# A two-layer window and differential attention encoder: first-layer input chunks 1 to 3 read in rows and turned on TensorE, and a planned wait of the mask step narrowed

## The chip, the core and the metric

The kernel runs on one core of a Trainium2 chip. The metric is the device time of one execution in microseconds; the time before is the median of 3 runs. The engines are TensorE (PE: matmuls and transposes; its weight loads are PEld), VectorE (DVE), ScalarE (ACT), GpSimd (POOL) and the queue of SyncE (SP), from which every DMA is issued in order.

## What is computed

Two sequences (1024 and 512 tokens, each with 16 meta tokens ahead, 1568 rows of 1024 together) pass through two layers. Cut to what matters:

```python
def layer(x, ...):
    h = rmsnorm(x, pre_g)                       # over the 1024 columns
    proj = h @ w_in                             # 3328 columns
    aq, ak, av, ag, bq, bk, bv, bg = split(proj)
    # A: 8 heads of 64, 2 key heads, window of +-128 tokens, meta keys, a sink
    oa = window_gqa_attention(rope(aq), rope(ak), av, sink) * silu(ag)
    # B: 4 heads, two softmaxes over all keys, p0 - lam * p1, then a norm
    ob = diff_attention(rope(bq), rope(bk), bv, lam, ...) * silu(bg)
    return x + rmsnorm(concat(oa, ob) @ w_out, post_g)
```

In the window attention the scores outside the window are masked with -1e30 ahead of the softmax.

## The kernel before

**Chunks and products.** The 1568 rows are cut into four chunks of up to 392 tokens (`ICH`; the copy of the 16 meta rows is left out). A product in full precision is three passes: each operand is split into a rounded part `hi` and a rest `lo`, and `hi*hi`, `lo*hi`, `hi*lo` are summed in one PSUM tile. `dense` makes one block of 128 output columns for one chunk: 8 slices of the contraction by 3 passes, 24 matmuls of up to 392 columns into `ps_d` (or `ps_o` where that is free). A head's input projection is four such blocks (`whl`, `whl`, `kk` and `vv` hold the first head's four weight blocks; the third is its values, the fourth its gate). `project` evicts each block with rope, split and DMA stores: `BS` (queries and keys), `BV` and `AV` (values in token rows, a quarter of a chunk on each partition range), `GT` (gates).

**Chunks of the first layer.** `load_x` reads every chunk from the transposed input `xT`, model dimension on the partitions. `start_stats` calls `prestats` for it: squares (ACT or POOL), sums on DVE, four PE transposes, a DVE reduction, two small POOL steps for the power -0.5, four more PE transposes (`rstd_bc`) and a copy to `rb`. `prenorm` then multiplies each of the eight slices by the gain and by `rb` on DVE (into `at`), and splits it: `hi` by a copy on ACT or DVE, `lo` by a subtraction on DVE. Chunk 0 goes another way: it is split without its norm, and `rb` is multiplied in at the eviction.

**Second layer.** `pre` works on token rows: `stat` sums squares on ACT, the rows are scaled, then groups of four PE transposes turn them into `ps_t`, and `hi` and `lo` come straight from that PSUM tile with the gain.

**Attention.** `attn_b` (B heads, four units) fills `ps_s` with scores, takes minima, exponentials and sums, transposes the probabilities (`pp` to `ps_t` to `at`) and multiplies by the values (`vv`). `attn_a` (two units) takes the heads in batches of three that share one `ps_s` tile of three banks; each head is two matmuls, then a DVE mask step (`tensor_tensor_reduce`: adds the mask and takes the minimum), an exponential and, per query block, `attn_a_tail`. Its result goes out as `MX`. `outproj` runs in steps (`OUT_ORDER`): `b` is the half of the products that needs only B heads, `s` and `S` the half that needs A heads, `p` the residual, `n` is `pre`.

**What sets the order.** Nothing is issued as written. `Recorder` notes every operation with what it reads and writes, and `schedule` is a list scheduler over the five engines with a priced duration for each operation: among the ready ones the smallest priority number goes first (`seq` less `boost` and `base`). An operation with two forms (`any`, `any_copy`) goes to the engine that is free. The engines then run these fixed orders, and the semaphores come from the data. `nc.extra` adds dependencies that only this planning sees. All instructions carry the helper's line (451 before, 448 after), so rows are told apart by their tiles.

Of the kernel before, what the change touches and what calls it, by code (L numbers as in the profile page):

```python
# [16 lines left out]
ALU = mybir.AluOpType  # L17
# [16 lines left out]
    [[(0, 392)], [(392, 392)], [(784, 256), (1056, 120)], [(1176, 392)]],  # L34
# [18 lines left out]
QUICK = 1  # L53
# [5 lines left out]
PRE_ACT = (0, 0, 0, 0, 0, 0, 0, 0)  # L59
# [4 lines left out]
ONLY = 4  # L64
# [478 lines left out]
def hymba_kernel(ctx, tc, xT, xr, w_in, w_out, rope, masks, pre_g, post_g, sub_g, sink_b, sink_m, lam_in, yo):  # L543
# [64 lines left out]
    def load_x(ci):  # L608
        xin[ci] = pair()
        nc.boost = START[f"x{ci}"] * 100000  # L610
        w = 2 if ci == 0 else 4
        for k in range(0, 8, w):
            o = 0
            for t0, m in ICH[0][ci]:
                dma(xin[ci][k // 4][:, k % 4:k % 4 + w, o:o + m],
                    xT.rearrange("(a p) t -> p a t", p=128)[:, k:k + w, t0:t0 + m])
                o += m
        nc.boost = 0
# [104 lines left out]
    def prestats(xs, tmp, n, only=False):  # L723
        if only:
            for i in range(4):
                r = slice(2 * (i % 2), 2 * (i % 2) + 2)
                x, y = xs[i // 2][:, r, 0:n], tmp[i // 2][:, r, 0:n]
                nc.any((nc.scalar, "activation", (y, x, AF.Square), {}),
                       (nc.gpsimd, "tensor_tensor", (y, x, x), dict(op=ALU.mult)))
                if i:  # L730
                    nc.vector.tensor_tensor(
                        tmp[0][:, 0:2, 0:n], tmp[0][:, 0:2, 0:n], tmp[i // 2][:, r, 0:n], op=ALU.add)
            nc.vector.tensor_tensor(tmp[0][:, 0, 0:n], tmp[0][:, 0, 0:n], tmp[0][:, 1, 0:n], op=ALU.add)
        else:
            for i in range(2):
                nc.scalar.activation(tmp[i][:, :, 0:n], xs[i][:, :, 0:n], AF.Square)
            nc.any_tt(tmp[0][:, :, 0:n], tmp[0][:, :, 0:n], tmp[1][:, :, 0:n], ALU.add)
            for k in (2, 1):
                nc.any_tt(tmp[0][:, 0:k, 0:n], tmp[0][:, 0:k, 0:n], tmp[0][:, k:2 * k, 0:n], ALU.add)
        return rstd_bc(tmp[0][:, 0, 0:n], n, 1.0 / D)  # L740

    def scaled(out, x, g, rb, n, act):
        for j in range(x.shape[1]):
            if act:
                nc.scalar.activation(out[:, j, 0:n], x[:, j, 0:n], AF.Copy, scale=g[:, j:j + 1])
                nc.any_tt(out[:, j, 0:n], out[:, j, 0:n], rb[:, 0:n], ALU.mult)
            else:
                nc.vector.scalar_tensor_tensor(
                    out[:, j, 0:n], x[:, j, 0:n], g[:, j:j + 1], rb[:, 0:n], op0=ALU.mult, op1=ALU.mult)

    def prenorm(l, ci, xs, rb, n):
        his, los = [], []
        for i in range(2):
            hi, lo = pair(F32R)
            for j in range(4):
                r = slice(j, j + 1)
                h = at_p([128, 1, CN])
                scaled(h, xs[i][:, r], preg[:, l, 4 * i + j:4 * i + j + 1], rb, n, PRE_ACT[2 * ci + i])
                h = h[:, :, 0:n]
                nc.any_copy(hi[:, r, 0:n], h)  # L760
                if l == 0 and ci < QUICK:
                    nc.vector.tensor_tensor(lo[:, r, 0:n], h, f32(hi[:, r, 0:n]), op=ALU.subtract)
                else:
# [834 lines left out]
```

## Time and profile before

| what | value |
|---|---|
| time, median of 3 runs (range) | 1935.77 us (1933.12 to 1939.91) |
| the profiled execution's own time | 1938.61 us |
| its span | 1936.8 us |
| PE busy | 1843.4 us, 95% of the span |
| DVE, ACT, POOL busy | 1515.2, 1008.1, 279.3 us |
| mean granted TensorE clock | 0.985 |

The profiled execution has its own time: 1.8 us of it lie outside the span. A sum made from the trace is a change against 1938.61, and is then taken from the median. A busy PE need not be PE at its peak, so durations of matmuls are read here from one start to the next. "Idle before" in a timeline is the wait just ahead of the row, with what ended it.

### The profile page before, as it was taken

The page shows a single profiled execution, that of the slowest core. Times are in us where ns is not written, and L with a number is a line of the kernel's source. Part 1 is how long each engine was busy: PE and PEld are TensorE (multiplying, and loading weights), DVE is VectorE, ACT ScalarE, POOL GpSimd, SP SyncE. Part 2 cuts the span into 40 slices and gives each one's busy share as a digit, 9 for nine tenths or more (in the row PEclk, how much of TensorE's full clock was granted, in tenths as well). Part 3 has the DMA queues.
Part 4 walks back from the last instruction along what each step waited for, and adds up shares of the span by engine and source line. Part 5 has one row for each costly group of instructions (what it writes and reads, how often), then busy time and mean ns, then how long its engine had stood idle before and what let it go on. Part 6 is the DMA issues. An engine that isn't in the chain of part 4 may idle for free.

```text
span 1936.8 us, 35552 instructions
## 1 busy us (share of the span) xinstructions
PE 1843.4 (95%) x12328; PEld 1771.3 (91%) x12328; DVE 1515.2 (78%) x3363; ACT 1008.1 (52%) x2417; POOL 279.3 (14%) x516
## 2 busy tenths in 40 slices
PE   6999999999999989999789999999999999999998
PEld 5989989999989889999789999999999999889998
DVE  8858788888787787587988397787967859869767
ACT  4335445454444475575765254454545438648632
POOL 3001111211121210000221021121111101101001
PEclk8999999999999999999989999999999999999999
DMA  7253363544543657556354535445353475684464
GB/s 252 56 161 105 110 170 102 148 119 109 153 117 108 154 144 198 118 133 178 120 196 116 152 100 160 120 118 161 98 167 114 124 180 125 159 229 99 109 205 150
DMA packets 299147, 273.02 MB, mean 141 GB/s; under 512 B 101560, under 2 KB 263480, under 8 KB 298840
## 3 DMA queue, kind: packets, MB, share of 16 engines
q1 hardware_dynamic: 298968, 270.75, 50.5%
q8 instruction: 98, 1.61, 0.4%
q14 instruction: 81, 0.66, 0.1%
HBM read 149.19 MB, written 96.01 MB: 127 GB/s over the span
## 4 chain that ended last, share of the span: by engine, by line
PE 70%; DVE 11%; DMA 8%; ACT 4%; issue 4%; SPq 2%; POOL 1%; DVEq 0%; POOLq 0%; ACTq 0%
PE ps_d L451 43%; PE ps_s L451 10%; PE ps_o L451 9%; PE ps_t L451 8%; DVE at L451 2%; DVE pp L451 2%; DVE slot L451 2%; ACT pp L451 2%; SPq L451 2%; DVE sm L451 1%; DMA vv<-BV 1%; DVE og L451 1%; DMA kk<-AK 1%; DVE ru L451 1%; POOL sm L451 1%
## 5 line engine op out<-in xcount | busy, mean ns | idle before, releaser
L451 PE MATMUL ps_d<-slot,whl 128*128 128x392 f32 (+2 forms) x4560 | 938.2, 347 | 15.0 <-ACT slot L451 6.7
L451 PEld LDWEIGHTS ps_d<-slot,whl 128*128 128x128 f32 x4560 | 785.7, 190 | 22.2 <-ACT slot L451 6.7
L451 PE MATMUL ps_s<-kk,qq 128*128 128x264 f32 (+9 forms) x1496 | 284.4, 319 | 21.7 <-ACT pp L451 5.7
L451 PE MATMUL ps_o<-at,vv 128*128 128x256 f32 (+6 forms) x1368 | 285.9, 307 | 8.4 <-DVE og L451 5.5
L451 ACT ACTIVATE at<-ps_t 128x256 fp32r<-128x256 f32 (+9 forms) x434 | 187.7, 439 | 202.7 <-PE ps_t L451 177.4
L451 ACT ACTIVATE pp<-ps_s,sm 116x1040 f32<-116x1040 f32 (+4 forms) x208 | 203.9, 980 | 169.9 <-DVE sm L451 161.5
L451 DVE TENSOR_TENSOR at<-ps_t,at 128x256 fp32r<-128x256 f32 (+6 forms) x472 | 224.5, 480 | 68.0 <-ACT at L451 53.5
L451 PEld LDWEIGHTS ps_s<-kk,qq 128*128 128x128 f32 (+4 forms) x1496 | 227.2, 185 | 46.9 <-ACT pp L451 9.0
L451 PE MATMUL ps_d<-whl,slot 128*128 128x256 f32 x1800 | 259.0, 288 | 8.6 <-DVE slot L451 6.0
L451 PEld LDWEIGHTS ps_d<-whl,slot 128*128 128x128 f32 x1800 | 235.1, 192 | 14.3 <-DVE slot L451 7.2
L451 DVE TENSOR_REDUCE sm<-ps_s 116x1 f32<-116x1040 f32 (+4 forms) x208 | 218.3, 1050 | 34.3 <-PE ps_s L451 33.3
L451 ACT ACTIVATE pp<-pp,sm 128x336 f32<-128x336 f32 (+6 forms) x347 | 206.6, 607 | 61.0 <-DVE sm L451 57.6
L451 PEld LDWEIGHTS ps_o<-at,vv 128*128 128x128 f32 (+1 forms) x1368 | 214.0, 190 | 16.8 <-ACT pp L451 5.4
L451 PE MATMUL ps_t<-ident,pp 128*128 128x128 f32 (+6 forms) x1248 | 203.5, 269 | 3.1 <-DVE at L451 1.6
L451 POOL TENSOR_TENSOR pad<-pp,pad 128x64 fp32r<-128x64 f32 (+3 forms) x145 | 53.2, 370 | 819.0 <-ACT pad L451 528.1
L451 PEld LDWEIGHTS ps_t<-ident,pp 128*128 128x128 f32 (+6 forms) x1248 | 147.8, 137 | 14.7 <-ACT pp L451 2.8
L451 DVE CUSTOM_DVE_ANT_0 pp<-ps_s,mk,nsinks 128x336 f32<-128x336 f32 (+2 forms) x192 | 97.1, 528 | 22.1 <-PE ps_s L451 20.3
L451 POOL TENSOR_TENSOR sm<-sm 128x2 f32<-128x2 f32 (+3 forms) x112 | 48.7, 437 | 408.2 <-DVE sm L451 404.6
L451 POOL TENSOR_TENSOR sm<-sm,mhalf 128x1 f32<-128x1 f32 (+7 forms) x98 | 80.8, 830 | 132.9 <-DVE sm L451 129.6
L451 ACT ACTIVATE og<-ps_o 64x128 f32<-64x128 f32 (+4 forms) x248 | 66.1, 287 | 44.8 <-PE ps_o L451 27.3
L451 ACT ACTIVATE ru<-ps_d 128x392 f32<-128x392 f32 (+5 forms) x100 | 48.7, 487 | 73.9 <-PE ps_d L451 64.2
L451 DVE TENSOR_TENSOR slot<-slot 128x512 f32<-128x512 f32 (+3 forms) x79 | 73.9, 945 | 8.4 <-ACT slot L451 8.0
(158 smaller groups left out, 2130.3 us busy)
## 6 DMA issues: line engine op xcount, KB each, us to landing
wraw<-in_w_in_dram SPq DMA_DIRECT2D x46, 512.0 KB
qq<-qq SPq DMA_DIRECT2D x144, 128.0 KB
BS<-st SPq DMA_DIRECT2D x80, 196.0 KB
qq<-AQ SPq DMA_DIRECT2D x96, 128.0 KB
gl<-GT SPq DMA_DIRECT2D x72, 128.0 KB
MX<-og SPq DMA_DIRECT2D x72, 128.0 KB
slot<-MX SPq DMA_DIRECT2D x11, 768.0 KB
kk<-BS SPq DMA_DIRECT2D x8, 1040.0 KB
```

Source lines behind the costliest of these rows:

```text
L451: fn(*[_real(a) for a in args], **{k: _real(a) for k, a in kw.items()})
```

## The change

Chunk 0 is loaded as before. Chunks 1 to 3 are read from `xr`, the input in token rows, as four tiles each of 96 or 98 rows by 1024 columns (chunk 3 into `pp` tiles, the others into `slot` tiles). Their norm is now `stat`, moved out of `outproj`: two ACT squares with a running sum per tile, one small DVE step and one POOL power; the rows are scaled in place (ACT or DVE). `turned`, which `pre` of the second layer now calls too, makes the transposes, `hi` and `lo`. Chunk 1 ends at 776 in place of 784, so that chunks 1 and 2 have 384 tokens (four times 96). In `attn_a` the line that made the planner hold the three mask steps of a batch until the batch's last matmul is gone. The planner's price of a DMA now follows the number of rows.

```diff
-    [[(0, 392)], [(392, 392)], [(784, 256), (1056, 120)], [(1176, 392)]],
+    [[(0, 392)], [(392, 384)], [(776, 264), (1056, 120)], [(1176, 392)]],
...
+        for v in (out, in_):
+            rows = [x for x in v.shape if x > 1] or [1]
+            nc.weight = max(nc.weight, cost * 16 // max(k for k in range(1, 17) if rows[0] % k == 0))
...
+            for j in range(4):
+                nc.stream = "x" if ci == 3 else "dense"
+                x = (p_p if ci == 3 else slot)([128, 2, 512])
...
+                    dma(x[a:b].rearrange("p u d -> p (u d)"), xr[t0:t0 + b - a])
...
+    def stat(parts, M):
+        r = sm_p([128, 4])
+        for u, p in enumerate(parts):
+            sq = ru_p([128, 512])
+            nc.scalar.activation(sq[0:M], p, AF.Square, scale=1.0 / 32, accum_out=r[0:M, u:u + 1])
+        nc.vector.scalar_tensor_tensor(
+            r[0:M, 2:3], r[0:M, 0:1], EPS, r[0:M, 1:2], op0=ALU.add, op1=ALU.add)
+        nc.gpsimd.tensor_tensor(r[0:M, 3:4], r[0:M, 2:3], mhalf[0:M, 0:1], op=ALU.pow)
+        return r[0:M, 3:4]
+
+    def turned(l, tiles, off, n):
+        his, los = [], []
+        for u in range(2):
+            hi, lo = pair(F32R)
+            for k in range(4):
+                pt = ps_t([128, 512])
+                o = 0
+                with nc.macro():
+                    for get, M in tiles:
+                        nc.tensor.transpose(
+                            pt[:, o:o + M], get(u)[:, 128 * k:128 * k + 128], ident[0:M, 0:M])
+                        o += M
+                g = preg[:, l, 4 * u + k:4 * u + k + 1]
+                p = pt[:, off:off + n]
+                nc.any_copy(hi[:, k, 0:n], p, g)
                 nc.vector.scalar_tensor_tensor(
...
+                    lo[:, k, 0:n], p, g, f32(hi[:, k, 0:n]), op0=ALU.mult, op1=ALU.subtract)
...
-                nc.extra = [nc.last]
                 for bi, (u, i) in enumerate(batch):
...
+            for x in xin[ci]:
+                r = stat([x[0:n // 4, u] for u in range(2)], n // 4)
+                for u in range(2):
+                    nc.any_copy(x[0:n // 4, u], x[0:n // 4, u], r)
```

PE in the first projection, before, after the matmuls of chunk 0 for all four blocks; `ps_t<-ident,slot` and `ps_t<-ident,sm` are the two groups of `rstd_bc`:

```order
L451 MATMUL ps_d<-slot,vv 128x392 x18
L451 MATMUL ps_t<-ident,ru 98x128 x4
L451 MATMUL ps_t<-ident,slot 98x128 x4
L451 MATMUL ps_t<-ident,sm 128x98 x4
L451 MATMUL ps_t<-ident,slot 94x128 x4
L451 MATMUL ps_o<-slot,whl 128x392 x3
```

The same place in the changed kernel; the groups of four or eight with `128x96` are the new transposes of chunk 1:

```order
L448 MATMUL ps_d<-slot,whl 128x392 x15
L448 MATMUL ps_t<-ident,sm 128x98 x4
L448 MATMUL ps_d<-slot,whl 128x392 x9
L448 MATMUL ps_o<-slot,kk 128x392 x12
L448 MATMUL ps_t<-ident,slot 128x96 x8
L448 MATMUL ps_o<-slot,kk 128x392 x12
L448 MATMUL ps_d<-slot,whl 128x384 x3
```

Chunk 1 now follows three blocks of chunk 0; the fourth block (`vv`) comes for all chunks behind chunk 3.

ACT at the start, before; `whl`, `kk`, `vv` from `pp` are the `hi` parts of the weights, `slot<-slot` the squares of chunks 0 and 1:

```order
L451 ACTIVATE slot<-slot 128x784 x3
L451 ACTIVATE slot<-slot,preg 128x392 x2
L451 ACTIVATE slot<-slot 128x784 x2
L451 ACTIVATE whl<-pp 128x1024
L451 ACTIVATE kk<-pp 128x1024
L451 ACTIVATE vv<-pp 128x1024
```

The same place on ACT in the changed kernel; `ru,sm<-slot` are the squares with their sums, `slot<-slot,sm` the scaling of rows:

```order
L448 ACTIVATE slot<-slot,preg 128x392 x2
L448 ACTIVATE ru,sm<-slot 96x512 x8
L448 ACTIVATE slot<-slot,sm 96x512
L448 ACTIVATE kk<-pp 128x1024
L448 ACTIVATE rb<-ps_t 128x392
L448 ACTIVATE slot<-slot,sm 96x512 x6
L448 ACTIVATE ru,sm<-slot 96x512
L448 ACTIVATE slot<-ps_t,preg 128x384 x2
```

Eight squares of chunk 1 stand ahead of the third weight block and of `rb`.

PE at the end of the first layer's attention, before; `ps_o<-at,vv` is the last product of the window attention, `ps_t<-ident,slot` are the transposes of `pre` for the second layer:

```order
L451 MATMUL ps_o<-at,kk 128x256
L451 MATMUL ps_d<-whl,slot 128x256 x3
L451 MATMUL ps_o<-at,vv 128x512
L451 MATMUL ps_d<-whl,slot 128x256 x12
L451 MATMUL ps_t<-ident,slot 128x128 x12
L451 MATMUL ps_d<-whl,slot 128x256 x30
```

The same place in the changed kernel:

```order
L448 MATMUL ps_o<-at,kk 128x256
L448 MATMUL ps_d<-whl,slot 128x256 x6
L448 MATMUL ps_o<-at,vv 128x512
L448 MATMUL ps_d<-whl,slot 128x256 x6
L448 MATMUL ps_d<-whl,at 80x256 x12
L448 MATMUL ps_d<-whl,slot 128x256 x12
```

150 output matmuls (eight short rows of three and one of 99 follow those shown) stand between the last product and the first transpose, where 12 stood; the transposes come behind them.

## Rows read from the trace of the kernel before

**Rows 1.** The page: engines over the span, last chain by engine, one group (busy, mean ns).
```profile
PE 1843.4 (95%) x12328; PEld 1771.3 (91%) x12328; DVE 1515.2 (78%) x3363; ACT 1008.1 (52%) x2417; POOL 279.3 (14%) x516
...
PE 70%; DVE 11%; DMA 8%; ACT 4%; issue 4%; SPq 2%; POOL 1%; DVEq 0%; POOLq 0%; ACTq 0%
...
L451 PE MATMUL ps_t<-ident,pp 128*128 128x128 f32 (+6 forms) x1248 | 203.5, 269 | 3.1 <-DVE at L451 1.6
```

**Rows 2.** Windows by stage: length, busy of each engine, granted clock, DMA.
```profile
0.00:119.00 119.00, 97.76 (x517) 92.70 (x517) 88.95 (x161) 43.52 (x72) 22.62 (x22) 0.94 0.54 170
...
650.00:962.00 312.00, 291.87 (x2119) 276.90 (x2119) 249.53 (x736) 203.68 (x584) 33.48 (x64) 0.98 0.58 148
962.00:1097.00 135.00, 120.38 (x788) 117.41 (x787) 94.26 (x176) 65.01 (x133) 21.43 (x29) 0.94 0.53 162
...
1850.00:1937.00 87.00, 74.57 (x599) 72.75 (x597) 60.84 (x97) 24.70 (x59) 10.84 (x12) 0.96 0.49 168
```

**Rows 3.** Timeline of PE, first stage: start, length, instructions, idle before.
```profile
9.05 7.27 PE L451 MATMUL ps_d<-slot,whl 128*128 128x392 f32 x22 [1.66 <-DVE slot L451]
...
40.28 0.91 PE L451 MATMUL ps_t<-ident,sm 98*128 98x98 f32 x4 [5.76 <-POOL sm L451]
...
44.81 1.18 PE L451 MATMUL ps_d<-slot,whl 128*128 128x392 f32 x3
45.79 1.18 PE L451 MATMUL ps_d<-slot,kk 128*128 128x392 f32 x3
...
60.70 4.53 PE L451 MATMUL ps_d<-slot,vv 128*128 128x392 f32 x24
65.06 0.68 PE L451 MATMUL ps_d<-slot,whl 128*128 128x376 f32 x3
...
73.29 0.60 PE L451 MATMUL ps_t<-ident,slot 128*98 128x128 f32 x4
73.64 0.76 PE L451 MATMUL ps_d<-slot,whl 128*128 128x376 f32 x3
...
118.69 0.28 PE L451 MATMUL ps_s<-kk,qq 128*116 128x264 f32 x1
```

**Rows 4.** Groups by form, 0 to 160 us: DVE steps of `prenorm` (busy, mean ns).
```profile
L451 DVE SCALAR_TENSOR_TENSOR at<-slot,preg,rb 128x392 f32<-128x392 f32 x16 | 9.2, 618 | 2.4 <-ACT rb L451 2.4
...
L451 DVE TENSOR_TENSOR slot<-at,slot 128x392 fp32r<-128x392 f32 x16 | 8.4, 557 | 0.3 <-ACT slot L451 0.2
```

**Rows 5.** Timeline of ACT near 945 us: one square with its sum, from `stat`.
```profile
944.98 0.62 ACT L451 ACTIVATE ru<-slot 128x512 f32<-128x512 f32 x1
945.50 0.18 ACT L451 ACTIVATION_READ_ACCUMULATOR ru<-slot 128x1 f32 x1
```

**Rows 6.** Windows of 1 us: a 98-row store of `BV`, then the 94-row stores.
```profile
47.00:48.00 1.00, 1.00 (x4) 1.00 (x4) 1.00 (x3) 0.91 (x3) 0.00 (x0) 0.50 0.87 256
96.00:97.00 1.00, 1.00 (x7) 1.00 (x7) 1.00 (x2) 0.00 (x0) 0.00 (x0) 1.00 0.14 48
```

**Rows 7.** Timeline of PE between the layers.
```profile
961.05 1.59 PE L451 MATMUL ps_d<-whl,slot 128*128 128x256 f32 x12
...
970.42 1.59 PE L451 MATMUL ps_t<-ident,slot 128*128 128x128 f32 x6 [7.57 <-ACT slot L451]
975.50 1.09 PE L451 MATMUL ps_t<-ident,slot 128*128 128x128 f32 x4 [3.49 <-DVE slot L451]
...
979.55 5.82 PE L451 MATMUL ps_d<-whl,slot 128*128 128x256 f32 x28 [1.16 <-DVE slot L451]
```

**Rows 8.** Timeline of SP: the store of the window attention's last result.
```profile
968.73 0.37 SPq L451 DMA_DIRECT2D MX<-og  x1
```

**Rows 9.** Timeline of PE, second layer's end.
```profile
1847.51 13.97 PE L451 MATMUL ps_d<-whl,slot 128*128 128x256 f32 x114
1863.14 0.38 PE L451 MATMUL ps_d<-kk,slot 128*128 128x256 f32 x1 [1.66 <-ACT kk L451]
```

**Rows 10.** Waits of DVE over the span: us, times, longest.
```profile
DVE pp L451 <- PE ps_s L451: 30.8, 19, 8.1
```

More of the change, by code (lines that the diff above doesn't have):

```diff
@@ L608, in load_x @@
     def load_x(ci):
-        xin[ci] = pair()
+        n = sum(m for _, m in ICH[0][ci])
         nc.boost = START[f"x{ci}"] * 100000
[L611 to L617, printed above, removed]
+        if ci == 0:
+            xin[0] = pair()
+            for k in range(0, 8, 2):
+                dma(xin[0][k // 4][:, k % 4:k % 4 + 2, 0:n],
+                    xT.rearrange("(a p) t -> p a t", p=128)[:, k:k + 2, 0:n])
+        else:
+            m = n // 4
+            cols = [t0 + i for t0, k in ICH[0][ci] for i in range(k)]
+            xin[ci] = []
+            for j in range(4):
+                nc.stream = "x" if ci == 3 else "dense"
+                x = (p_p if ci == 3 else slot)([128, 2, 512])
+                a = 0
+                while a < m:
+                    t0, b = cols[m * j + a], a
+                    while b < m and cols[m * j + b] == t0 + b - a:
+                        b += 1
+                    dma(x[a:b].rearrange("p u d -> p (u d)"), xr[t0:t0 + b - a])
+                    a = b
+                nc.stream = "dense"
+                xin[ci].append(x)
         nc.boost = 0
@@ L721, in rows @@
         return [t[:, j] for t in tiles for j in range(k)]
[L723 to L739, printed above, removed]
-        return rstd_bc(tmp[0][:, 0, 0:n], n, 1.0 / D)
@@ L742, in scaled, with prestats @@
[L742 to L747, printed above, removed]
-                nc.vector.scalar_tensor_tensor(
[L749 to L763, printed above, removed]
-                    nc.any_tt(lo[:, r, 0:n], h, f32(hi[:, r, 0:n]), ALU.subtract)
+    def prestats(xs, tmp, n):
+        for i in range(4):
+            r = slice(2 * (i % 2), 2 * (i % 2) + 2)
+            x, y = xs[i // 2][:, r, 0:n], tmp[i // 2][:, r, 0:n]
+            nc.any((nc.scalar, "activation", (y, x, AF.Square), {}),
+                   (nc.gpsimd, "tensor_tensor", (y, x, x), dict(op=ALU.mult)))
+            if i:
+                nc.vector.tensor_tensor(
+                    tmp[0][:, 0:2, 0:n], tmp[0][:, 0:2, 0:n], tmp[i // 2][:, r, 0:n], op=ALU.add)
+        nc.vector.tensor_tensor(tmp[0][:, 0, 0:n], tmp[0][:, 0, 0:n], tmp[0][:, 1, 0:n], op=ALU.add)
+        return rstd_bc(tmp[0][:, 0, 0:n], n, 1.0 / D)
@@ L765, in prenorm @@
             his.append(hi)
             los.append(lo)
-        hT[ci] = (rows(his, 4), rows(los, 4))
+        return rows(his, 4), rows(los, 4)
+    def prenorm(ci):
+        n = sum(m for _, m in ICH[0][ci])
+        m = n // 4
+        hT[ci] = turned(0, [(lambda u, x=x: x[0:m, u], m) for x in xin[ci]], 0, n)
     def load_w(src, pool=None, pri=0):
@@ L1466, in pre @@
                 return
[L1467 to L1485 removed]
+            tiles = []
+            for x in range(4):
+                i = 3 * ci + x
+                M = 128 if i < 12 else 80
+                tiles.append((lambda u, i=i, M=M: xv(i // 3, u, i % 3, M), M))
+            hT[ci] = turned(l + 1, tiles, 8 * ci, CN)
         steps = dict(b=first, s=second, S=lambda *c: second(*c, keep=False), f=fetch, p=post, n=pre, l=load, g=gains)
@@ L1496, in start_stats @@
     def start_stats(ci):
-        rb0[ci] = prestats(xin[ci], pair(), sum(m for _, m in ICH[0][ci]), ci < ONLY)
+        n = sum(m for _, m in ICH[0][ci])
+        if ci == 0:
+            rb0[0] = prestats(xin[0], pair(), n)
+        else:
+            for x in xin[ci]:
+                r = stat([x[0:n // 4, u] for u in range(2)], n // 4)
+                for u in range(2):
+                    nc.any_copy(x[0:n // 4, u], x[0:n // 4, u], r)
     his, los = [], []
@@ L1521, in hymba_kernel @@
         if ci:
-            prenorm(0, ci, xin[ci], rb0[ci], sum(m for _, m in ICH[0][ci]))
+            prenorm(ci)
     units = [(range(10 + 4 * h, 14 + 4 * h), lambda l, h=h: attn_b(l, h)) for h in range(4)]
```

31 lines of the change are left out of this document (removed).

## The prediction

> **What bounds the kernel now.** The page comes first: PE is busy for 95% of the span and holds 70% of the last chain [rows 1]. So the change can move the time in two ways only: the work that PE gets, and the 93 us in which it is not busy, with the stretches at a lowered clock. The windows by stage show where those lie [rows 2]: 21 us of idle PE before the first score at 118.7 us, 20 us in the first layer's window attention (650 to 962), 15 us between the layers, 12 us in the last stage; the two long stages of B heads that aren't shown hold 17 us in 1024. The mean granted clock is 0.94 in the first stage and 0.94 between the layers: some of each ran at the lower level.
>
> The timeline of PE gives the unit prices. 24 matmuls of 392 columns take 65.06 - 60.70 = 4.36 us, 0.182 us each; at the lower level three take 0.98 us, 0.327 each; four transposes take 73.64 - 73.29 = 0.35 us, 0.088 each [rows 3]. A matmul of 256 columns is 13.97 / 114 = 0.1225 us [rows 9].
>
> **Work added on PE.** Each of three chunks gets 8 groups of 4 transposes and loses the 8 of its norm: 96 - 24 = 72 more, by 0.088 us +6.3 us. The number of columns that the matmuls pass is unchanged, since the chunks still hold 1552 tokens. Upper bound: the mean busy time of one transpose, 0.269 us [rows 1], which counts overlap twice and would hold for transposes that stand alone, gives +19.4. Below +6.3 it goes only if they fall into idle time, and that is counted with the stages.
>
> The Trainium skill speaks against the small price: "TensorE: Matmul & The Clock Gate", section "Part 4: PE-mode transpose", states about 275 ns for a full transpose inside a kernel. By that the term would be 72 x 0.275 = 19.8 us. The row of four in 0.35 us disagrees with that for transposes that stand in fours, as these do; by that rule the rival on transposes below would hold.
>
> **The first stage.** Before, 468 dense matmuls and 48 transposes precede the first score. From PE's start at 9.05 us they need 468 x 0.182 + 48 x 0.088 = 89.4 us, to 98.5; it came at 118.69 [rows 3], so 20 us were lost: 3.3 because the first 22 matmuls took 7.27 us where 4.0 would do, some 9 between 33 and 44 us while chunk 1's norm was made on DVE and POOL (5.76 of it in one wait), 3 to the lower level behind that, the rest in small waits. In the changed order 390 matmuls and 120 transposes precede the first score; the other 78 come later and are no loss.
>
> What goes: DVE's share of a chunk's norm. Per chunk 8 multiplications of 0.618 and 8 subtractions of 0.557 [rows 4] with about 4 us of sums become 8 `lo` steps of 0.62 and some small ones, from 13.5 to about 7 us. With that the long wait at 40 us should go, since the rows of chunk 1 are ready by about 28 us. What comes: ACT gets 8 squares of 0.62 + 0.18 us per chunk [rows 5], 6.4 us, with scalings of rows and `hi` copies some 15 us per chunk, against 12.8 us of matmuls and 2.8 of transposes on PE. ACT and PE are then even, and what is queued behind the squares on ACT (the `hi` of the third weight block, `rb`, the evictions of chunk 0) waits for chunk 1's rows. My list for the changed stage: 3 for the first pacing, 2 for the second weight block (24 matmuls stand in front of it in place of 33), 3 around `rb` and the third block, 4 for ACT's pace in chunks 1 and 2, 4.5 for the fourth block; all but the first are estimates from these durations and the order. That block's raw weights wait for a `pp` tile that holds chunk 3, and its `lo` stands on DVE behind a rope of five steps (2 x 0.62, 4 x 0.56) that needs the last matmuls of the block before: about 3.5 us and the split itself with only the transposes of the third block as cover. Sum 16.5 against 20: **-3.5 us**. Ends: -13 if ACT keeps up and the fourth block is covered, +8 if ACT paces PE by twice as much.
>
> **The 94-row stores.** A 98-row store moved 256 GB/s at a DMA share of 0.87, the stores in pieces of 94 and fewer rows 48 GB/s at 0.14 [rows 6]. Chunk 2 now has 96 rows to a tile. PE rarely waited for those stores: **-1 us** (0 to -3). What the stores of 96 rows cost no row shows; the 98-row one is the nearest.
>
> **Between the layers.** After the last product of the window attention PE did 12 matmuls, then waited 7.57, 3.49 and 1.16 us and once more for 1 [rows 7]. The first two waits are for rows of the residual; the matmuls at 979.55 wait for the last window result, stored at 968.73 [rows 8] and loaded again: 18.4 us after the last product. The 12 transposes and first matmuls ran at the lower level, some 4 us lost. In the changed order 150 output matmuls stand there instead of 12, and by their tiles 102 of them (6 of an early chunk, 24 of the meta tile, 72 of chunk 2) do not need that last result: 102 x 0.1225 = 12.5 us of cover against 12 x 0.1225 = 1.5. I take **-11 us** of these 13.2 and the 4 us of the lower level: some wait for the last result stays. Ends: -16, and -2 if DVE, which is busy for most of that stretch, holds the evictions of the cover.
>
> **Second layer's end.** 114 matmuls covered the last weights and 1.66 us were missing, some 2 more behind [rows 9]; the changed order has 153: **-3 us** (0 to -4).
>
> **The mask step.** The removed line binds only the planner; a mask step's semaphore waits for its own head's matmuls either way. What it can give is an earlier place. DVE waited 30.8 us in 19 waits for scores [rows 10], and two thirds of a batch's matmuls, about 0.7 us, could be taken off each: 13 us of DVE's wait, in stages where PE is busy for 94% [rows 2]. The planner used it: from the first masked score to the last product the first layer now has 1248 dense matmuls in place of 1329, 9.4 us less cover, the second 939 for 999, 7.2 us less. If the stage is bound by PE, it gets shorter by that and nothing is lost; if by its own chain, PE idles there instead. I take **0** (-3 to +16.6): a PE at 94% is nearer to the first.
>
> **Sum.** +6.3 - 3.5 - 1 - 11 - 3 + 0 = -12.2 us: the profiled execution would go from 1938.6 to 1926.4, the median of 1935.8 to about 1923.5.
>
> **Rivals.**
> *The cover only moved.* The mask step has its data no sooner where it counts, the window stages last as long as before, and the 16.6 us come back as idle PE there: 1923.5 + 16.6 = 1940, no change that can be measured. For it: DVE is busy 250 of 312 us in that stage and has its own waits. Against: PE is the busier one.
> *A first stage at the lower level.* If the rows of chunk 1 land late, ACT stands in its eight squares, the third weight block behind them, and PE gets gaps as long as the one at 34 to 40 us, behind which it ran at the lower level. If chunks 1 and 2 run so, 144 x (0.327 - 0.182) = +20.9 us: 1944, slower. It decides from gaps of about 6 us on; for it speaks ACT's even load, against it that PE has two weight blocks of chunk 0 in hand.
> *Transposes at their full length.* 19.4 in place of 6.3, +13.1 us: 1936.6, no change. It needs groups that do not overlap with the matmuls around them, against the 0.35 us for four.
> *More than that.* The window stages do get shorter and the first stage runs clean: -9 and -3 more, 1911.
>
> **How the numbers follow.** Forecast 0.52, cover moved 0.20, lower level 0.10, full transposes 0.05, more 0.13. A measurement of this kernel tells 0.3%, 5.8 us, from no change. Nearly all of the forecast and the best case lie below 1930, with a little of the moved cover: faster 0.64; the rest of that and the transposes: same 0.23; slower 0.13. The range of 8 in 10 leaves out the far ends of the best and the worst case: 1909 to 1940.
>
> **What would show it.** The first score near 106 us with no wait over 4 us on PE before 60 us; granted clock 1.00 there; the wait of 7.6 us between the layers gone, with the second layer's transposes behind the output matmuls; 12400 PE instructions; the window stages shorter by about 9 and 7 us at the same idle share. Wrong would be: idle PE in the window stages above 30 us, or a first stage in which PE waits for ACT.

## The result, and the profile after

The changed kernel takes 1956.74 us (median of 4, 1953.72 to 1965.6) against 1936.96 us of the kernel before on the same chip: the ratio is 1.0111, 95% interval 1.0071 to 1.0151. It is slower by about 20 us; 1923.5 had been forecast, and the time lies above the range. The profiled execution took 1953.72 us, with a span of 1951.9, so that what follows from the two traces accounts for 15 of the 20 us.

The page of the changed kernel, engines and one group (busy, mean ns, idle before it, what ended most of that):

```profile
PE 1856.2 (95%) x12400; PEld 1776.0 (91%) x12400; DVE 1486.9 (76%) x3326; ACT 1034.0 (53%) x2478; POOL 273.4 (14%) x528
...
L448 PE MATMUL ps_s<-kk,qq 128*128 128x264 f32 (+9 forms) x1496 | 288.1, 319 | 34.6 <-DVE sm L448 16.4
```

The same group in the page of the kernel before:

```profile
L451 PE MATMUL ps_s<-kk,qq 128*128 128x264 f32 (+9 forms) x1496 | 284.4, 319 | 21.7 <-ACT pp L451 5.7
```

Against [rows 1] PE is busy for 12.8 us more, and the score matmuls now wait for `sm`, which the mask steps write. Where the time went is read by stage. The windows of the changed kernel, cut at its own first score, first masked score, last product of the window attention and the same three of the second layer (length, busy of PE, PEld, DVE, ACT, POOL, granted clock, DMA):

```profile
0.00:103.80 103.80, 87.83 (x511) 82.97 (x511) 64.98 (x139) 57.38 (x118) 13.05 (x23) 0.98 0.64 184
103.80:640.50 536.70, 529.40 (x3444) 511.31 (x3444) 423.81 (x809) 263.92 (x554) 89.73 (x181) 1.00 0.45 124
640.50:945.20 304.70, 283.55 (x2036) 265.41 (x2035) 235.87 (x706) 192.66 (x558) 33.10 (x72) 0.99 0.56 145
945.20:1102.30 157.10, 143.81 (x937) 139.01 (x937) 107.85 (x196) 75.24 (x162) 23.95 (x29) 0.97 0.51 155
1102.30:1590.00 487.70, 480.08 (x3123) 464.66 (x3122) 383.96 (x751) 244.21 (x517) 75.63 (x158) 1.00 0.49 134
1590.00:1856.70 266.70, 247.43 (x1679) 231.22 (x1678) 207.47 (x625) 172.99 (x505) 27.04 (x53) 0.98 0.53 134
1856.70:1944.70 88.00, 84.11 (x681) 81.41 (x679) 59.40 (x95) 26.20 (x61) 9.98 (x11) 1.00 0.57 194
```

Four stages of before answer to [rows 2]; here are its two stages of B heads and its second window stage, cut in the same way:

```profile
118.70:649.60 530.90, 518.13 (x3376) 498.36 (x3374) 426.10 (x807) 257.86 (x546) 92.12 (x182) 1.00 0.45 124
...
1097.30:1589.10 491.80, 488.24 (x3179) 473.98 (x3177) 385.95 (x757) 239.02 (x511) 73.42 (x161) 1.00 0.48 133
1589.10:1847.70 258.60, 249.72 (x1738) 236.21 (x1737) 208.20 (x630) 172.85 (x511) 25.35 (x47) 0.99 0.57 148
```

A stage's length alone misleads, since the new orders move dense matmuls between stages. With 0.182 us for a matmul of 392 columns [rows 3] and 0.1225 for one of 256 [rows 9], what each stage lost beyond its work is:

| stage | length, before to after | dense matmuls moved | their time | change of the loss |
|---|---|---|---|---|
| to the first score | 118.7 to 103.8 | -78 | -14.2 (and +4.4 for transposes) | -5.1 |
| B heads, layer 1 | 530.9 to 536.7 | +68 | +12.4 | -6.6 |
| window attention, layer 1 | 311.6 to 304.7 | -81 | -9.3 | +2.4 |
| between the layers | 136.1 to 157.1 | +141 | +20.3 | +0.7 |
| B heads, layer 2 | 491.8 to 487.7 | -54 | -9.8 | +5.7 |
| window attention, layer 2 | 258.6 to 266.7 | -59 | -7.1 | **+15.2** |
| the last stage | 80.9 to 88.0 | +63 | +7.7 | -0.6 |

With the 4.4 us of transposes and 1 us less behind PE's end the column gives the 15.1 us by which the spans differ. "Loss" is the length of a stage less the time of its dense matmuls; each row rests on one execution of either kernel. The first layer's start won more than forecast; the second layer's window stage got 8 us longer with 7 us less to do.

### The profile page after: what moved, and what is told of

Its sections match the earlier page's. It is cut to its first block, busy times and chain, and to the rows that moved or that the text cites. A ratio compares the mean times of both kernels' runs of the same rounds, so it can differ in the third digit from the quotient of the medians.

```text
span 1951.9 us, 35786 instructions
## 1 busy us (share of the span) xinstructions
PE 1856.2 (95%) x12400; PEld 1776.0 (91%) x12400; DVE 1486.9 (76%) x3326; ACT 1034.0 (53%) x2478; POOL 273.4 (14%) x528
## 5 line engine op out<-in xcount | busy, mean ns | idle before, releaser
L448 ACT ACTIVATE at<-ps_t 128x256 fp32r<-128x256 f32 (+12 forms) x443 | 191.2, 437 | 200.2 <-PE ps_t L448 173.5
L448 PE MATMUL ps_t<-ident,pp 128*128 128x128 f32 (+6 forms) x1280 | 209.1, 270 | 3.3 <-DVE at L448 2.1
L448 POOL TENSOR_TENSOR pad<-pp,pad 128x64 fp32r<-128x64 f32 (+4 forms) x151 | 56.4, 379 | 772.8 <-ACT pad L448 426.2
L448 POOL TENSOR_TENSOR sm<-sm 128x2 f32<-128x2 f32 (+2 forms) x112 | 47.9, 428 | 478.5 <-DVE sm L448 447.7
L448 ACT ACTIVATE ru<-slot 128x512 f32<-128x512 f32 (+1 forms) x82 | 51.1, 624 | 56.8 <-DVE slot L448 54.7
```

The source lines that it names most:

```text
L448: fn(*[_real(a) for a in args], **{k: _real(a) for k, a in kw.items()})
```

## Experiments

All times are medians; each ratio stands to the kernel before on the same chip, with its 95% interval. The runs were made on several chips, so ratios are the safer comparison between them; they are not quotients of the medians and differ from these by up to 3 us. The lengths of stages are those of the one profiled execution, whose time lies up to 7 us from the median (1934.76 in e3, 1932.18 in e7, 1964.45 in e4). "Rows" is the new input of chunks 1 to 3, "wait" the planner's rule that a batch's mask steps follow its last matmul.

| run | rows | wait, layer 1 / 2 | us | ratio (95%) | window stage, layer 1 / 2, us |
|---|---|---|---|---|---|
| e1 | yes | in / in | 1942.13 | 1.0010 (0.9996 to 1.0025) | 325.2 / 258.5 |
| e2 | no | out / out | 1959.37 | 1.0107 (1.0083 to 1.0132) | 302.5 / 264.4 |
| e3 | yes | out / in | 1941.95 | 1.0017 (1.0000 to 1.0034) | 306.6 / 258.1 |
| e4 | yes | in / out | 1958.45 | 1.0106 (1.0076 to 1.0136) | 323.7 / 266.2 |
| e5 | yes | out / out, regrouped | 1967.66 | 1.0151 (1.0125 to 1.0177) | 310.9 / 273.7 |
| e6 | yes | out / in, regrouped | 1946.45 | 1.0037 (1.0021 to 1.0053) | 314.3 / 257.7 |
| e7 | no, price only | in / in | 1938.22 | 1.0001 (0.9986 to 1.0017) | 316.6 / 259.5 |
| e8 | yes | out / out, reset in 2 | 1952.88 | 1.0081 (1.0049 to 1.0113) | 308.8 / 262.3 |
| e9 | yes | in / in, reset in 2 | 1942.10 | 1.0016 (1.0003 to 1.0029) | 327.0 / 249.7 |
| e10 | yes | in / in, reset in 1 | 1939.53 | 1.0005 (0.9991 to 1.0019) | 320.6 / 259.2 |
| e11 | yes | out / in, reset in both | 1927.83 | 0.9939 (0.9918 to 0.9961) | 310.5 / 252.7 |
| e12 | yes | out / out, planner told | 1934.47 | 0.9962 (0.9947 to 0.9978) | 296.5 / 252.3 |
| e13 | no | out / in, reset in both | 1936.00 | 0.9978 (0.9962 to 0.9994) | 310.8 / 255.5 |
| e14 | yes | in / in, reset in both | 1935.35 | 0.9982 (0.9968 to 0.9995) | 322.3 / 253.2 |
| e15 | yes | out / out, told, reset in 1 | 1930.85 | 0.9966 (0.9947 to 0.9986) | 310.3 / 251.5 |

**Which part, and in which layer (e1 to e4).** e2 takes the line out of the kernel before. e1, e3 and e4 put it back into the changed kernel: for both layers, for the second only, and for the first only.

```diff
-                nc.extra = [nc.last]
```
```diff
+                nc.extra = [nc.last]
```
```diff
+                nc.extra = [nc.last] if l != 0 else []
```
```diff
+                nc.extra = [nc.last] if l != 1 else []
```

> The changed kernel with the planner's wait of the mask steps put back in both layers; the input in rows, the transposes and the DMA price stay. On PE its order is that of the changed kernel up to the first score of the window attention (640.5 us there, 649.6 before) and, apart from shifts of a few matmuls, that of the kernel before from there on. Theory A, the mask step's place costs the time: the run keeps the 9 us gained by 640 us and loses no more than before behind it: about 1927 us, and PE's waits of ps_s on DVE sm are back at about 2 us. Theory B, the rows and their 72 transposes cost it: about 1950 to 1957 us. Theory C, each new order wins or loses at random: anything between, with waits spread over all stages.

> The kernel before with only the planner's wait of the mask steps taken out; chunks come transposed as before. PE's order is that of the kernel before up to 649.6 us, and from the second layer on that of the changed kernel. Theory A: about 9 us worse than the changed kernel, since it lacks the gain of the first stages: 1960 to 1966 us, with about 16 us of PE's ps_s waiting for DVE sm. Theory B: 1930 to 1936 us, no change. Theory C: anything between.

> The changed kernel with the wait put back in the second layer only. On PE it is the changed kernel up to the window attention of the second layer (1590 us) and about that of the kernel before in it. From the traces, the stretch from there to PE's end lost 14 to 15 us against before. Theory A, the mask step's place acts in each layer's window stage: about 1940 us, with the ps_s waits on DVE sm left in the first layer (about 6 us). If instead the loss of the second layer was handed on from the first layer (later data, another clock), it stays and the time is 1952 to 1957 us.

> The changed kernel with the wait put back in the first layer only: PE's order is that of the run with the wait back in both layers up to the second layer's window attention, and about that of the changed kernel in it. Theory A: the time of that run plus 14 to 15 us: about 1941 us, with about 10 us of ps_s waits on DVE sm, all behind 1590 us. Handed on from the first layer: about 1927 us.

The second layer's edit costs 15 to 16 us: 1942.1 to 1958.5 (e1 to e4), and 1942.0 to 1956.7 (e3 to the changed kernel); by the ratios it is 18 to 19 us. The first layer's costs nothing beside the rows (e1 to e3, e4 to the changed kernel). e3 came as theory A has it, e2 just under its range, e4 by its step. e1 missed by 15 us: it has its 9 us at 641 us, and loses them in the first window stage. Its window there:

```profile
641.00:966.20 325.20, 302.09 (x2118) 285.35 (x2119) 253.18 (x735) 195.30 (x572) 38.02 (x69) 0.95 0.56 143
```

PE does what it did before (x2118 against x2115) in 13.6 us more, at a granted clock of 0.95 against 0.98 [rows 2]: 302.1 us busy in place of 291.5, and 3 more idle.

**The waits inside a batch (e5, e6).** The trace of the changed kernel shows what the edit does to a batch of three heads. PE, then DVE, in the second layer's first batches (start, length, instructions, idle before; the first PE row is the matmuls of two heads, the second those of the third):

```profile
1593.44 0.73 PE L448 MATMUL ps_s<-kk,qq 128*128 128x272 f32 x4
1594.77 0.57 PE L448 MATMUL ps_s<-kk,qq 128*128 128x336 f32 x2 [0.60 <-DVE sm L448]
...
1594.20 0.50 DVE L448 CUSTOM_DVE_ANT_0 pp<-ps_s,mk,nsinks 128x272 f32<-128x272 f32 x1 [1.30 <-PE ps_s L448]
1594.63 0.08 DVE L448 DVE_READ_ACCUMULATOR2_ANT sm<- 128x1 f32 x1
1595.38 0.57 DVE L448 CUSTOM_DVE_ANT_0 pp<-ps_s,mk,nsinks 128x336 f32<-128x336 f32 x1 [0.67 <-PE ps_s L448]
```

The same batch before:

```profile
1592.14 1.03 PE L451 MATMUL ps_s<-kk,qq 128*128 128x272 f32 x6
...
1593.21 0.50 DVE L451 CUSTOM_DVE_ANT_0 pp<-ps_s,mk,nsinks 128x272 f32<-128x272 f32 x1 [1.26 <-PE ps_s L451]
...
1593.64 0.56 DVE L451 CUSTOM_DVE_ANT_0 pp<-ps_s,mk,nsinks 128x336 f32<-128x336 f32 x1
...
1594.13 0.57 DVE L451 CUSTOM_DVE_ANT_0 pp<-ps_s,mk,nsinks 128x336 f32<-128x336 f32 x1
```

The third head's matmuls start at 1594.77, 0.06 us after the first head's mask step has written its minimum (1594.71), though that step reads another bank of the tile and writes nothing that they read. The second head's matmuls end at 1594.17, but its mask step starts at 1595.38, 0.04 us after the third head's (1595.34). So matmuls and mask steps of one tile wait for one another, whichever heads they belong to: 3.0 us from the first matmul to the last mask step's end, where 2.6 were enough. In the programs it stands as a wait for DVE on the third head's matmul; before, there is none:

```
before   MATMUL ps_s_19514<-kk_19153,qq_19436 128x336 x2
changed  MATMUL ps_s_19624<-kk_19243,qq_19546 128x336 [waits DVE_49]
```

In the program of the changed kernel 32 of the 68 batches have such a wait (15 and 17 by layer; the expectation below says 15 and 18), in that of the kernel before none. In the trace 24 of them held PE up. Over the second window stage (waits of PE: us, times, longest) the changed kernel shows

```profile
PE ps_s L448 <- DVE sm L448: 10.1, 15, 2.4
PE ps_s L448 <- DMA kk<-AK: 3.7, 2, 2.8
```

and the kernel before has no wait of `ps_s` for `sm` there. e5 and e6 leave every engine's order alone and emit a batch's matmuls ahead of its mask steps (`i` is the place of the batch's first mask step, `z` that of its last matmul; what hits goes to `move`, the rest to `stay`):

```diff
+            part = order[i:z + 1]
...
+                hit = (o is first or (o.eng in engs) or any(d in move for d in o.deps)
+                       or any(x.pool in frees for x in o.new))
...
+                order[i:z + 1] = stay + move
...
-        for o in self.schedule():
+        for o in self.regroup(self.schedule()):
```

> The changed kernel with the same order of instructions on every engine. Only the program order between engines differs: where a mask step stood between the matmuls of its own batch (15 batches in the first layer, 18 in the second), the whole batch's matmuls are now emitted ahead of it. In the changed kernel the last head's matmuls of these 33 batches carry a wait for a mask step of an earlier head, which writes nothing that they read and reads another bank of the same tile; here they carry none, and the mask steps wait for the batch's last matmul instead. Theory A1, that wait on the shared tile is what costs: PE's waits of ps_s on DVE sm fall from 16.4 us (24 waits) to 3 or less, and the time from 1956.7 to 1940 to 1946 us. Theory A2, the moved cover costs, whoever waits for whom: PE idles as long in the same places for something else, DVE's waits for scores grow by about as much, and the time stays at 1952 to 1958 us.

> The kernel with the planner's wait taken out in the first layer only (1942 us), with the same change of program order: its 15 waits of a batch's last matmuls on an earlier mask step (6.3 us in 9 waits in its trace) are gone, every engine's order is as it was. Theory A1: 4 to 7 us less, 1935 to 1938 us, no slower than the kernel before. Theory A2: 1940 to 1944 us.

Both theories missed: e5 is 11 us slower than the changed kernel (8 by the ratios, whose intervals overlap) and e6 4.5 us slower than e3 (4 by the ratios, likewise). Second window stage of e5, window and waits (the helper stands in line 487 there):

```profile
1594.40:1868.10 273.70, 247.80 (x1678) 231.66 (x1677) 206.16 (x625) 172.32 (x504) 25.89 (x53) 0.97 0.53 130
```
```profile
PE ps_t L487 <- DVE at L487: 6.4, 6, 2.1
PE ps_s L487 <- DMA kk<-AK: 5.8, 2, 4.9
PE ps_d L487 <- DVE ru L487: 3.1, 4, 1.1
PE ps_s L487 <- DVE sm L487: 3.0, 4, 1.9
```

The waits for `sm` fall to 3.0 us and come back larger behind the later mask steps. An order that counts on early mask steps is not mended by taking its waits away.

**A control (e7).** Only the three lines of the DMA price are added to the kernel before:

```diff
+        for v in (out, in_):
+            rows = [x for x in v.shape if x > 1] or [1]
+            nc.weight = max(nc.weight, cost * 16 // max(k for k in range(1, 17) if rows[0] % k == 0))
```

> The kernel before with only the planner's new price of a DMA. What is computed and every instruction stay; the orders of the first layer differ, and from the second layer on they are those of before. With the input in rows the price changes no engine's order at all. This sizes what a mere reordering does. If orders of the same work are worth the same: 1934 to 1941 us, and a window stage of the first layer at 309 to 314 us. If the first layer's window stage hangs on the order dealt, as the 325 and 324 us with the wait back against 311.6 us before suggest: it lies 5 us or more away from 311.6, and the granted clock there away from 0.98.

No change in time, as the first reading has it; the window stage, 5.0 us away from 311.6 at the same clock of 0.98, fits neither reading well. The stages do move: the first masked score comes at 639.8 us, 10 us early as with the rows (2 of them because 12 dense matmuls fewer stand ahead of it). Only the sum of the stages tells a gain.

**Cover or mask steps (e8, e9).** Priorities of the window units decide how much dense work lies between their steps. e8 alters them in the changed kernel, e9 in e1:

```diff
-BASE_A = ((-200, 1500, 1500, -200, 200, 400), (0, 0, 0, 0, 1500, 0))
+BASE_A = ((-200, 1500, 1500, -200, 200, 400), (0,0,0,0,0,400))
```
```diff
-BASE_A = ((-200, 1500, 1500, -200, 200, 400), (0, 0, 0, 0, 1500, 0))
+BASE_A = ((-200, 1500, 1500, -200, 200, 400), (0, 0, 0, 0, 1500, 800))
```

> The changed kernel with the priorities of the second layer's window units set to 0 and 400 in place of 1500 and 0. Its first layer's orders are those of the changed kernel, the wait stays out; 974 dense matmuls stand in the second window stage in place of 939, 27 more ahead of it and 617 in place of 680 behind it. 19 of its batches have a wait for a mask step in their middle, 18 in the changed kernel. Theory A2, that stage lasts as long as its chain and the taken cover is lost: the stage stays at 260 to 267 us, the last stage falls from 88 to about 79 us, the one before grows by 5: 1948 to 1953 us. If PE bounds the stage: it grows with its work, and the sum stays at 1955 to 1959 us.

> The kernel with the wait back in both layers (1942.1 us), with the priority of the second layer's last window unit set to 800 in place of 0: 954 dense matmuls in the second window stage in place of 998, 662 in place of 617 behind it, and no mask step between the matmuls of its batch. It takes cover away without touching the mask steps' rule. Theory A2 in its plain form (a chain of fixed length): the stage stays at 258 us, the last one grows by 5 to 6 us: 1946 to 1949 us. If PE bounds the stage with the wait in place: it shrinks by 5 us and the time stays at 1940 to 1944 us; then the loss of 16 us in the changed kernel is the mask steps' own, and not that of the cover.

The last two stages of e9:

```profile
1598.40:1848.10 249.70, 241.01 (x1693) 228.00 (x1692) 207.41 (x625) 171.08 (x510) 28.18 (x49) 1.00 0.57 145
1848.10:1933.80 85.70, 81.59 (x664) 79.08 (x662) 59.14 (x94) 26.37 (x61) 9.93 (x11) 1.00 0.56 194
```

With the wait in place the stage shrinks by 8.8 us with 44 matmuls less, the last one grows by 7.7, and the time stays: PE bounds it, and moved cover costs nothing. With the wait out, 35 matmuls more than in the changed kernel don't lengthen the stage (262.3 us in e8, the last one 79.2, the one before 5.8 longer, as theory A2 has it). The stage of e8, cut in the same way:

```profile
1603.50:1865.90 262.40, 247.30 (x1715) 229.75 (x1714) 210.57 (x623) 171.96 (x511) 26.10 (x54) 1.00 0.55 144
```

It has 15.1 us of idle PE for 19.3, so the added matmuls fill waits; but it also ran at a clock of 1.00 for 0.98, and the intervals of its ratio and the changed kernel's overlap. That the stage lasts as long as its chain there is argued, not shown. What e9 shows does not need it: against e9, which has about the changed kernel's cover, the mask steps' order costs 266.7 - 249.7 = 17.0 us: 10.6 of idle PE (10.1 by the waits for `sm`) and 6.4 of busy time with 14 instructions less, at a clock of 0.98 for 1.00. No wait for `sm` stands in that stage of e9. The lowered clock hangs only in part on the waits for mask steps (last section).

**What the planner knew (e12).** The changed kernel, with one rule added to the planner: a score matmul or a mask step is not dealt before those of the other kind already dealt for its tile have ended.

```diff
+            if o.batch is not None:
+                at = max([x.t1 for x in busy.get(o.batch, []) if x.kind != o.kind], default=0.0)
+                at += self.SYNC_TO[e]
+                if at > t + 1e-9 and at > self.SYNC_TO[e]:
+                    return at
```

> The changed kernel, the wait out in both layers, with a planner that knows of the waits inside a batch: a score matmul isn't dealt before the mask steps already dealt for its tile are done, nor a mask step before the tile's matmuls already dealt. 13 batches of the second layer still get a mask step in their middle (18 in the changed kernel), cover there is 936 matmuls (939). If the planner's ignorance is the cause: the second window stage at 250 to 260 us with less than 3 us of ps_s waits on DVE sm, and 1940 to 1946 us. If dealing mask steps into the middle of a batch is bad whatever the planner knows: that stage at 262 us or more, and 1950 us or more.

22 us come back (29 by the ratios), and the kernel is faster than the one before by 0.4%; the time came under the first reading's range (1940 to 1946), the stage within it (250 to 260). Both window stages of e12, and the longest waits of PE in the second:

```profile
640.30:936.80 296.50, 279.96 (x2007) 264.42 (x2008) 233.11 (x703) 189.35 (x561) 25.58 (x59) 0.98 0.57 147
...
1579.70:1832.00 252.30, 242.55 (x1675) 227.21 (x1674) 206.94 (x622) 171.63 (x502) 30.74 (x58) 0.99 0.56 141
```
```profile
PE ps_d L458 <- DVE ru L458: 3.3, 4, 2.3
PE ps_d L458 <- DVE slot L458: 2.9, 4, 1.3
```

No wait for `sm` is left in that stage, with 936 dense matmuls in it (939 in the changed kernel). Its program still has 13 batches there with a mask step ahead of some of their matmuls, 11 with a wait for it (21 and 17 in the changed kernel). Early mask steps are not bad in themselves; dealing them without counting the waits that the shared tile brings is. Whether three tiles in place of one would take the waits away was not run.

**What the rows are worth (e10, e11, e13 to e15).** These runs set priorities anew, on the kernels that the table names. Given are the last two numbers of each layer in `BASE_A`, which were 200, 400 in the first and 1500, 0 in the second: e10 has 800, 400 in the first; e11 -200, 800 and 1500, 400; e13 the same, made from the kernel before with its transposed input and its old price of a DMA; e14 800, 400 and 1500, 400; e15 has 800, 800 in the first and the planner of e12.

> The kernel with the wait back in both layers (1942.1 us), with the priority of the first layer's first window unit set to 800 in place of 200. Orders differ in the first layer's window stage and just ahead of it; 1338 dense matmuls there in place of 1332, the second layer is dealt as before. In that stage the kernel with the wait back took 325 us at a clock of 0.95, the kernel before 311.6 at 0.98 with the same work. If that loss belongs to the order that the new start happened to get: 310 to 315 us at 0.97 or more, and 1928 to 1933 us in all. If it follows from the input in rows (an earlier arrival at the stage, say): 320 to 326 us again, and 1939 to 1944 us.

> The input in rows, the wait out in the first layer only (1942 us), and the window units' priorities set anew: -200 and 800 in the first layer (200 and 400 before), 1500 and 400 in the second (1500 and 0). The first window stage holds 1301 dense matmuls in place of 1248, the stage behind it 687 in place of 792; the second has 966 in place of 1001, 650 in place of 617 behind it. If cover in the first window stage and a shorter stage behind it are worth their matmuls: 1930 to 1937 us. If what counts is which order is dealt: anywhere from 1930 to 1950 us.

> The faster kernel of the last series (1927.8 us: rows, wait out in the first layer only, priorities set anew) with the input transposed as before in chunks 1 to 3. From the first layer's window stage on its PE order is nearly that kernel's (1292 dense matmuls in that stage in place of 1301, all later stages alike); ahead of it, it is that of the kernel before. If the input in rows is worth what the first two stages show (640.5 against 649.6 us): 1935 to 1939 us. If that gain is given back later whatever the order, as with the wait back: 1926 to 1930 us.

> The input in rows, the wait in both layers, priorities 800 and 400 in the first layer, 1500 and 400 in the second: the kernel of 1939.5 us with the second layer's setting of the kernel of 1927.8 us. If that one's gain sits in the second layer (A1 and the last stage 333 us against 336 to 337): 1935 to 1937 us. If it needs the wait out in the first layer (448 us from the first masked score to the second layer's first score, against 457 in the kernel of 1939.5): no lower than 1935. Below 1930 both would be wrong, and the wait in the first layer would cost nothing.

> The kernel whose planner is told of the waits inside a batch (1934.5 us), with the first layer's window priorities at 800 and 800 in place of 200 and 400. The first window stage then holds 1301 dense matmuls and the stage behind it 687, as in the kernel of 1927.8 us; the second holds 944. If the gain of the told planner and that of the first layer's setting add: 1922 to 1928 us. If they are the same gain (cover in the first window stage): 1930 to 1936 us.

e11 and e13 have almost the same order from the first window stage on and differ in the input. Their windows up to there, e11 first:

```profile
0.00:105.80 105.80, 87.17 (x510) 82.30 (x510) 65.00 (x139) 57.42 (x118) 12.11 (x23) 0.98 0.64 181
105.80:642.50 536.70, 529.71 (x3444) 511.55 (x3445) 424.00 (x809) 264.61 (x555) 89.55 (x181) 1.00 0.45 124
```
```profile
0.00:119.00 119.00, 97.37 (x516) 92.42 (x517) 88.33 (x161) 43.18 (x72) 21.88 (x22) 0.94 0.54 170
119.00:651.70 532.70, 519.80 (x3377) 499.43 (x3375) 426.52 (x807) 258.26 (x546) 92.31 (x182) 0.99 0.45 123
```

9.2 us are won by the first masked score, and 8.2 of them are there in the end: 1927.8 against 1936.0 (7.6 by the ratios, as the two ran on different chips). So the rows are worth about 8 us against the transposed input as e13 deals it. Against every order of that input this is not shown: e7, with the new price of a DMA, brought it to the first masked score at 639.8 us too, and e13 was not run with that price. e11 came 2 us under its first range and beats both kernels, by 0.6% against the one before. With the wait in the first layer the 8 us are given back: the first window stage took 325, 324, 327, 321 and 322 us in e1, e4, e9, e10 and e14, under two different settings, where the transposed input has 311.6 (316.6 in e7). e10 says that this is not one unlucky order; what it is stays open. In e1 10.6 of the 13.6 us are busy time at a lower clock, but in e10 and e14 the clock of that stage is 0.98, as before, so the clock alone is not the answer. e14 gets its gain in the second layer as expected. e15 shows that the told planner and the new first-layer setting are mostly one gain (1930.9; by the ratios no faster than e12).

## Why the prediction was wrong, point by point

- **The mask step, 0 (-3 to +16.6): here it failed.** It measures +15 to +16 us in the second layer (e1 to e4), 0 in the first beside the rows. The step that fell is "a mask step's semaphore waits for its own head's matmuls either way". The rows at 1594.77 and 1595.38 show both sides of it wrong: the mask step waits for the tile's later matmuls, and these for it. The line was the planner's only record of that. Its upper end had nearly the right size for another reason, cover; that was luck. The choice "bound by PE" holds for that stage with the wait in place (e9), but PE's share there is not 94%: it is busy for 249.7 of 258.6 us, 97%, and the list of idle PE at the prediction's head leaves these 8.9 us out.
- **The rival of the moved cover** named the right stage and 16.6 us, and predicted 1940; its mechanism fell with e9, where moved cover cost nothing, and with e12, which has the changed kernel's cover.
- **The first stage, -3.5:** right, at -5.1. The first score came at 103.8 us (forecast 106), 103 to 108 in the other kernels with rows; the longest wait ahead of 60 us is 1.66 us at 17.77, the mean clock is 0.98 for 0.94, and once PE runs, ACT holds it up once, for 1.27 us. The rival of a lower level did not come. Its "gaps of about 6 us" are too long a measure, though: the last section has the clock falling behind waits of 1.4 to 2.8 us. (The rope of "five steps" is priced as six.)
- **Transposes, +6.3:** too high. The changed kernel's first stage has the longest wait of the bullet above, and four transposes of 96 rows with the matmuls behind them:

```profile
17.77 0.64 PE L448 MATMUL ps_t<-ident,slot 128*98 128x128 f32 x4 [1.66 <-DVE slot L448]
...
47.94 0.49 PE L448 MATMUL ps_t<-ident,slot 96*128 96x96 f32 x4
48.21 0.77 PE L448 MATMUL ps_o<-slot,whl 128*128 128x384 f32 x3
```

  48.21 - 47.94 is 0.27 us for four, 0.0675 each: 96 x 0.0675 - 24 x 0.088 = +4.4 us. That row is at the low end: all 24 new groups of the stage took 0.07 to 0.08 us for each transpose, 0.073 on average, which makes +4.9. The 275 ns of the Trainium skill ("TensorE: Matmul & The Clock Gate", "Part 4: PE-mode transpose") agree with the length of a single transpose in the trace, 269 ns on average [rows 1], and not with what one adds in these groups. The rival built on full lengths is out.
- **What was missed in the rows' favour:** the first layer's B heads lost 6.6 us less than before (the table above). No step had this stage; the rows' part of the sum, +6.3 - 3.5 - 1 = +1.8 us, measures +4.4 - 5.1 - 6.6 = -7.3 in the traces, and -8.2 between e13 and e11. No run separates the stores' -1.
- **Between the layers, -11:** it measures +0.7, outside its ends. (The 150 output matmuls counted there are 153.) The wait of 7.57 us [rows 7] did go; it belongs to the mask edit, not to the rows, since e1 has one of 7.68. In its place stand nine waits, the longest of 3.9 us, for evictions and sums on DVE, which has no room there. The changed kernel from 945 to 1020 us, waits, then windows of 10 us:

```profile
PE ps_d L448 <- DVE slot L448: 11.3, 9, 3.9
```
```profile
950.00:960.00 10.00, 7.93 (x42) 7.43 (x42) 9.27 (x16) 3.76 (x11) 2.22 (x2) 0.66 0.46 148
960.00:970.00 10.00, 8.23 (x66) 7.76 (x65) 9.92 (x16) 7.39 (x18) 3.67 (x2) 1.00 1.02 321
...
1010.00:1020.00 10.00, 5.62 (x31) 4.76 (x30) 9.53 (x22) 7.85 (x18) 3.35 (x6) 0.93 0.64 207
```

  That is the case of its low end (DVE holds the evictions of the cover). The working counted matmuls of cover, not the DVE steps that each needs.
- **Cover taken from the B heads:** of the 141 matmuls that came between the layers 81 left the window stage ahead and 54 the second layer's B heads behind, and these lost 5.7 us (7.6 us of idle PE for 3.6). No step had looked there.
- **Second layer's end, -3:** -0.6.
- **The window stages "shorter by about 9 and 7 us at the same idle share":** the first did so (-6.9 us, and -9.1 in e2, with 21 and 18.5 us of idle PE for 20), the second got 8.1 longer. Idle PE in both together was 40 us, which the prediction had named as the sign of its being wrong.

Put together, in the trace: -12.2 us had been forecast. The rows gave 9 us more than their steps said, the gain between the layers did not come (+12), nor that at the end (+2), the second layer's B heads lost 6 and the two window stages 15 and 2: +16. With 1 us less behind PE's end that is the trace's 15. All but the rows' part comes with the one line that "binds only the planner", since e2, which has no other edit, repeats these stages.

## What to carry to other kernels

A dependency that exists only in a planner may be the record of a wait that the chip really makes, here through a tile shared by three heads; before it is removed, look in the new program for the waits that take its place, or teach them to the planner, as e12 did. Whether a stage is bound by PE or by its chain is told by moving cover alone (e9), not by PE's share of 94%. Cover for a wait is worth no more than the engine that has to evict it can take.

## What the runs showed of the hardware

Some waits came with a loss beyond their length, and most of the short ones did not. In the second window stage PE idled 10.6 us more than in e9, and ran the same kind of work for 6.4 us longer at a lower mean clock. In windows of 10 us the granted clock of that stage is 1.00 but for 1700 to 1710, 1720 to 1740 and 1740 to 1750 us, which together lack 5.1 us of full clock. These are the three places, windows, then the waits ahead of them:

```profile
1700.00:1710.00 10.00, 8.35 (x46) 7.51 (x45) 6.74 (x15) 4.91 (x15) 1.32 (x3) 0.83 0.76 206
```
```profile
1725.00:1730.00 5.00, 2.24 (x11) 2.21 (x11) 0.99 (x4) 0.56 (x2) 0.00 (x0) 0.85 1.11 231
1730.00:1735.00 5.00, 4.97 (x26) 4.68 (x25) 1.43 (x5) 2.32 (x6) 0.00 (x0) 0.81 1.00 276
...
1745.00:1750.00 5.00, 4.47 (x24) 4.14 (x25) 4.00 (x14) 3.70 (x13) 0.00 (x0) 0.66 0.63 191
```
```profile
1703.03 0.66 PE L448 MATMUL ps_t<-ident,pp 128*128 128x128 f32 x4 [1.40 <-DVE at L448]
...
1727.79 0.47 PE L448 MATMUL ps_s<-kk,qq 128*128 128x208 f32 x2 [2.76 <-DMA kk<-AK]
...
1745.05 0.58 PE L448 MATMUL ps_s<-kk,qq 128*128 128x336 f32 x2 [2.35 <-DVE sm L448]
```

Behind each of these waits part of the next stretch ran at the lower of the two levels. Only the third is a wait for a mask step; the 14 others for `sm`, of 0.43 to 0.67 us, left the clock at 1.00. Not every long wait lowered it: one of 1.91 us at 1670.73 did not, nor one of 2.17 us for a DMA at 1748.45 in e8. e2, which has the same order in that stage, repeats all three places, behind waits of 1.40, 2.20 and 2.34 us for the same three things; so they come with the order. How the first two follow from the mask steps is not shown.

A wait of a matmul for a mask step ends within 0.06 us of the step's last write, all 24 times: the cost lies in the order, not in the handing over.
